# A two-layer hybrid trunk on one core: weight splits further ahead, and work queued in another order

## The chip, the cores and the metric

The kernel runs as one program on one core of one Trainium2 chip. The metric is the device time of one execution in microseconds (us). The kernel before takes 1798.98 us, the median of 3 runs (1797.5 to 1801.09). The engines are TensorE (PE for matmuls, PEld for its weight loads), VectorE (DVE), ScalarE (ACT), GpSimd (POOL) and SyncE (SP), which issues the transfers here. Every engine works through its own list of instructions in order.

## What is computed

Two layers over 512 tokens of width 1024, all in float32. Cut to what matters:

```python
for l in range(2):
    sh1, sc1, gt1, sh2, sc2, gt2 = split(silu(c) @ w_mod[l] + b_mod[l])
    h = rms_norm(x, g_pre1) * (1 + sc1) + sh1
    gu, gv, q, k, v, qi, ki, wi, lx, lg = split(h @ w_in)
    y_a = gelu(gu) * (block_mix(layer_norm(gelu(gv))) + b)     # gMLP, blocks of 128
    y_b = attention(rope(q), rope(k), v, keys=top128(indexer(qi, ki, wi)))
    y_c = gelu(lg) * linear_recurrence(causal_conv4(lx))        # RG-LRU
    g_a, g_b, g_c = split(sigmoid(h @ w_gate + b_gate))
    merged = g_a * (y_a @ w_br[0]) + g_b * (y_b @ w_br[1]) + g_c * (y_c @ w_br[2])
    x = x + gt1 * rms_norm(merged @ w_o, g_post1)
    h2 = rms_norm(x, g_pre2) * (1 + sc2) + sh2
    z_g, z_v = split(causal_conv3(h2 @ w_up))                   # 2816 + 2816 columns
    x = x + gt2 * rms_norm((silu(z_g) * z_v) @ w_down, g_post2)
```

## The kernel before

**Units of weights.** The tokens stand in four blocks (`TB`) of 128. All weights come as a stream of 143 units for each layer, each a tile of 128x1024, in the order of `unit_names` (L39): 4 `lx`, 4 `qi`, 1 `ki`, 4 `lg`, 4 `gv`, 4 `gu`, the 12 of `branch(2)`, 4 `v`, 4 pairs of `k` and `q`, the 12 of `branch(0)`, the 12 of `branch(1)`, 8 `wo`, 44 `up`, 22 `dn`. A branch has two `gate` units and one `br` unit, four times.

**Split products.** A product in float32 is made of three matmuls (`mm3`, L128 to L132): both operands are split into a rounded high part and the rest, and high x high (L130), high x low (L131) and low x high (L132) are summed in PSUM, with weights and activations in either role. A unit is 24 such matmuls. The weights' split is made on the way: `W.conv` (L162) has ACT copy the landed tile `wst` to `wh` (L109) and DVE subtract it, giving `wl` (L112). `W.get` (L191) emits the splits up to `LA` = 3 units ahead of the unit it hands out; there are `RB` = 5 pairs of buffers and 6 landing tiles. All other tiles of 128x512 (`S`, L93) come from one pool of `NS` = 46. Activations are split in the same way into `hh` and `hl` or two `S` tiles.

**Background work.** Between units the code calls `B.pump` (L213), a slot: it lets generators emit a few instructions each. Those are the recurrence (`lru`), the indexer with its top-k search (`indexer`, L519: rounds of MAX8 at L560 and MATCH_REPLACE8 at L562, then the ties and one last bias tile), the gMLP mixing, the attention (`attention`, L674), the modulation rows of later phases (`mod_task` and `mod_fin`, L299 and L321, among the "low" tasks) and the next layer's small parameters (`prepare`). A generator that yields -n isn't called again for n slots. `B.drain` (L232) pumps until nothing is left; it stands before the first `br` unit of `branch(1)`, which needs the attention's result, and at the end of the layer's two halves.

**Attention.** 16 steps (head, block), one a slot. `score` (L678) is a matmul, a masked maximum on DVE (L685), an Exp on ACT (L106) and a scaling on POOL (L116); `flip` (L697) is the transposes on PE (L702) and a copy to `S` on ACT (L109); `values` (L707) the matmuls with `v`. In slot n the code emits score n, then flip n-2, then values n-3. The score of block i needs the indexer's bias i; the last one, bias 3, is the longest search.

**Token phases.** `wo` and `dn` (`tok_phase`, L397) hold all eight PSUM banks. Their last `TAIL` = 8 units are gone through token block by token block, so that a block's chain of norms (`chain`, L440: two sums of squares on ACT, `rsqrt` on POOL at L240, DVE for the rest) lies beside the next block's matmuls. For that, 8 units must be split at once: `W.conv` fills `wh`/`wl`, and `W.extra` splits three more into `S` tiles; then the activations that the tail needs are split (`hl_of`). After the last block, five units of the next phase are begun for half of the tokens (`start_half`, L373), between them the transposes of blocks 2 and 3 (`norm_out`, L354), then finished.

**Startup.** ACT sums the squares of `x`'s four blocks, and for each DVE and POOL make the factor; DVE accumulates the modulation row `acc` from eight tiles `m` (`mod_acc`, L293: L116 and L121).

## Time and profile before

| | us |
|---|---|
| median of 3 runs | 1798.98 |
| the profiled execution | 1798.2 |
| its span | 1796.4 |
| PE busy | 1720.5 (96%) |
| DVE busy | 1111.9 (62%) |
| ACT busy | 711.3 (40%) |
| POOL busy | 323.5 (18%) |

A matmul's bar covers the pipeline's depth, so the busy time of PE says that it nearly always has work, not that it runs at its peak. An idle time in the timeline stands in brackets with what ended it. PEclk is the granted clock of TensorE as a share of full speed; its mean over the run is 0.983. At full clock the 512-column matmuls of a unit follow each other every 0.227 us, at half clock every 0.427 us. Line numbers are those of the kernel before.

### The profile page before, as it was taken

The page shows a single profiled execution, that of the slowest core. Times are in us where ns is not written, and L with a number is a line of the kernel's source. Part 1 is how long each engine was busy: PE and PEld are TensorE (multiplying, and loading weights), DVE is VectorE, ACT ScalarE, POOL GpSimd, SP SyncE. Part 2 cuts the span into 40 slices and gives each one's busy share as a digit, 9 for nine tenths or more (in the row PEclk, how much of TensorE's full clock was granted, in tenths as well). Part 3 has the DMA queues.
Part 4 walks back from the last instruction along what each step waited for, and adds up shares of the span by engine and source line. Part 5 has one row for each costly group of instructions (what it writes and reads, how often), then busy time and mean ns, then how long its engine had stood idle before and what let it go on. Part 6 is the DMA issues. An engine that isn't in the chain of part 4 may idle for free.

```text
span 1796.4 us, 20845 instructions
## 1 busy us (share of the span) xinstructions
PE 1720.5 (96%) x7972; PEld 1421.0 (79%) x7972; DVE 1111.9 (62%) x1631; ACT 711.3 (40%) x1087; POOL 323.5 (18%) x248
## 2 busy tenths in 40 slices
PE   3999999899999999999999899998999999999998
PEld 1877888688889788888787688876888888888876
DVE  6738798844466888563465578986445676445442
ACT  3484323433343334342335643243333344334331
POOL 3241101632000112110003201044200012111000
PEclk8899999999999999999999999999999999999999
DMA  8424334432423666333234253444224153333311
GB/s 333 141 83 163 126 125 140 138 118 71 139 85 120 187 211 189 103 110 103 71 118 129 94 166 116 134 148 128 94 76 170 59 179 126 102 98 94 112 53 47
DMA packets 67643, 224.57 MB, mean 125 GB/s; under 512 B 7636, under 2 KB 8020, under 8 KB 67416
## 3 DMA queue, kind: packets, MB, share of 16 engines
q1 hardware_dynamic: 67248, 223.10, 38.8%
q8 instruction: 62, 1.02, 0.2%
q14 instruction: 37, 0.30, 0.1%
q10 hardware_dynamic: 296, 0.14, 0.0%
HBM read 219.02 MB, written 4.19 MB: 124 GB/s over the span
## 4 chain that ended last, share of the span: by engine, by line
PE 72%; DVE 12%; ACT 7%; issue 3%; DMA 3%; POOL 1%; SPq 0%; ACTq 0%; DVEq 0%; POOLq 0%
PE ps L132 23%; PE ps L131 23%; PE ps L130 23%; DVE wl L112 3%; PE ps L126 3%; DVE acc L121 2%; DVE s L121 2%; ACT s L104 2%; ACT s L109 2%; ACT wh L109 2%; DVE s L112 2%; POOL s L112 1%; DMA s<-in_rows_dram 1%; ACT L104 1%; DVE m L560 1%
## 5 line engine op out<-in xcount | busy, mean ns | idle before, releaser
L130 PE MATMUL ps<-hh,wh 128*128 128x512 f32 (+1 forms) x1608 | 606.0, 377 | 2.2 <-ACT wh L109 2.2
L132 PE MATMUL ps<-hh,wl 128*128 128x512 f32 (+1 forms) x1608 | 601.8, 374 | 2.9 <-DVE wl L112 2.8
L131 PE MATMUL ps<-hl,wh 128*128 128x512 f32 (+1 forms) x1608 | 601.4, 374 | 2.4 <-DVE hl L112 2.4
L112 DVE TENSOR_TENSOR wl<-wst,wh 128x1024 fp32r<-128x1024 f32 x273 | 350.2, 1286 | 317.5 <-ACT wh L109 315.9
L132 PEld LDWEIGHTS ps<-hh,wl 128*128 128x128 f32 x1608 | 303.2, 189 | 59.0 <-DVE wl L112 5.0
L131 PEld LDWEIGHTS ps<-hl,wh 128*128 128x128 f32 x1608 | 303.3, 189 | 57.1 <-DVE hl L112 3.4
L130 PEld LDWEIGHTS ps<-hh,wh 128*128 128x128 f32 x1608 | 303.5, 189 | 56.5 <-ACT wh L109 3.1
L109 ACT ACTIVATE wh<-wst 128x1024 fp32r<-128x1024 f32 x274 | 286.2, 1051 | 142.2 <-PE ps L132 104.8
L112 POOL TENSOR_TENSOR s<-s,s 128x512 f32<-128x512 f32 (+1 forms) x126 | 218.4, 1741 | 545.1 <-DVE s L121 422.5
L121 DVE SCALAR_TENSOR_TENSOR s<-ps,lw,s 128x511 f32<-128x511 f32 (+3 forms) x208 | 154.7, 747 | 92.6 <-ACT s L104 89.0
L130 PE MATMUL ps<-wh,s 128*128 128x512 f32 x384 | 151.1, 394 | 4.1 <-ACT s L109 4.1
L132 PE MATMUL ps<-wh,s 128*128 128x512 f32 x384 | 151.0, 393 | 2.2 <-DVE s L112 2.2
L131 PE MATMUL ps<-wl,s 128*128 128x512 f32 x384 | 151.1, 394 | 0.4 <-DVE wl L112 0.4
L104 ACT ACTIVATE s<-ps,lw 128x512 f32<-128x512 f32 x112 | 83.2, 761 | 131.9 <-PE ps L132 131.8
L240 POOL TENSOR_TENSOR sm<-sm,mhalf 128x1 f32<-128x1 f32 x40 | 22.4, 561 | 513.7 <-DVE sm L118 483.6
L109 ACT ACTIVATE s<-s 128x512 fp32r<-128x512 f32 (+2 forms) x100 | 59.9, 617 | 112.1 <-DVE s L112 65.0
L104 ACT ACTIVATE s<-ps,bg 128x512 f32<-128x512 f32 x48 | 33.0, 688 | 155.7 <-PE ps L132 155.7
L121 DVE SCALAR_TENSOR_TENSOR acc<-ms,cact,acc 128x1024 f32<-128x1024 f32 x70 | 93.5, 1336 | 0.0
L130 PEld LDWEIGHTS ps<-wh,s 128*128 128x128 f32 x384 | 72.9, 190 | 20.1 <-ACT s L109 5.0
L132 PEld LDWEIGHTS ps<-wh,s 128*128 128x128 f32 x384 | 72.9, 190 | 18.2 <-DVE s L112 3.1
L104 ACT ACTIVATE s<-s 128x512 f32<-128x512 f32 x52 | 32.4, 631 | 136.8 <-DVE s L121 136.7
L131 PEld LDWEIGHTS ps<-wl,s 128*128 128x128 f32 x384 | 72.7, 189 | 16.4 <-DVE wl L112 1.3
(128 smaller groups left out, 1937.4 us busy)
## 6 DMA issues: line engine op xcount, KB each, us to landing
wst<-in_wu_dram SPq DMA_DIRECT2D x286, 512.0 KB, 3.8
ms<-in_wm_dram SPq DMA_DIRECT2D x80, 512.0 KB, 4.0
s<-in_rows_dram SPq DMA_DIRECT2D x34, 256.0 KB, 6.1
m<-in_wm_dram SPq DMA_DIRECT2D x16, 512.0 KB, 8.5
s<-in_x_dram SPq DMA_DIRECT2D x16, 256.0 KB, 5.6
xd<-s SPq DMA_DIRECT2D x8, 256.0 KB, 2.0
s<-xd SPq DMA_DIRECT2D x8, 256.0 KB, 6.3
out_dram<-s SPq DMA_DIRECT2D x8, 256.0 KB, 2.1
```

The lines of the kernel that those rows point to most:

```text
L104: A_.activation(o, i, f, bias=bias, scale=scale)
L109: A_.activation(o, i, AF.Copy, scale=scale)
L112: (eng or V).tensor_tensor(o, a, b, op)
L121: V.scalar_tensor_tensor(o, a, s, b, op0=op0, op1=op1)
L126: T_.matmul(o, l, r, start=start, stop=stop)
L130: T_.matmul(o, lh, rh, start=start, stop=False)
L131: T_.matmul(o, lh, rl, start=False, stop=False)
L132: T_.matmul(o, ll, rh, start=False, stop=stop)
L240: G_.tensor_tensor(y, h, mhalf, ALU.pow)
L560: V.max(m, cur[:, :n])
```

## The change

`RB` goes to 6, `LA` to 5 and `NS` to 42. The four `v` units and their copies to `S` stand right behind `ki`, ahead of `lg`. Attention emits flip and values of a slot ahead of its score, and a score waits until slot `at + 4` (it was 3) and two slots behind the emission of its bias. The split of `ya`, which was four ACT copies and four POOL subtractions in one go ahead of `branch(0)`, is a background task of ACT and DVE, one each two slots. In the token phases' tails activation splits and weight splits alternate; `sumsq` is cut in two, and the second half (`rstd`, on DVE and POOL) is queued behind one more weight split in `chain`; the same cut in the startup puts two steps of `acc` ahead of the four `rstd`. The low tasks pause while half units are carried; `mod_fin` and `lru` start later by two slots and one, `prepare` by up to twelve; Silu of a gate tile is queued behind the second convolution. The code of `lg` and of the two loads for gMLP is the same behind the `v` units and left out below.

```diff
@@ -39,6 +39,7 @@
 def unit_names():
     n = [("lx", j) for j in range(4)]
     n += [("qi", j) for j in range(4)] + [("ki", 0)]
+    n += [("v", t) for t in range(4)]
     n += [("lg", j) for j in range(4)]
     n += [("gv", t) for t in range(4)] + [("gu", j) for j in range(4)]
...
     n += branch(2)
-    n += [("v", t) for t in range(4)]
     for j in range(4):
         n += [("k", j), ("q", j)]
...
-    RB = 5
-    LA = 3
-    NS = 46
+    RB = 6
+    LA = 5
+    NS = 42
...
-        def add(self, gen, first=False):
-            self.tasks.insert(0 if first else len(self.tasks), [gen, 0])
+        def add(self, gen, first=False, wait=0):
+            self.tasks.insert(0 if first else len(self.tasks), [gen, self.slot + wait])
 
         def pump(self, budget):
             self.slot += 1
-            if self.low and self.slot % self.every == 0:
+            if self.low and not carry and self.slot % self.every == 0:
...
+    carry = []
     B = Bg()
...
     def mod_fin(l, v, key, acc):
-        yield -2
+        yield -4
...
@@ -337,6 +338,9 @@
         s = small(2)
         for i, a in enumerate(srcs):
             act(junk, a, AF.Square, acc=s[:, i:i + 1])
+        return s
+
+    def rstd(s):
         h = small(1)
         ts(h, s[:, 0:1], s[:, 1:2], D * EPS, AD, AD)
         return rsqrt(h)
...
         W.hold = W.cur
-        W.conv(W.cur + RB)
-        W.extra(TAIL - RB)
         W.aside = TAIL - RB
-        a_, w_ = [], []
-        for k in range(nk - TAIL, nk):
-            a_.append(hl_of(k))
-            w_.append(W.take())
+        a_ = []
+        for k in range(TAIL):
+            a_.append(hl_of(nk - TAIL + k))
+            if W.ncv < W.cur + RB:
+                W.conv(W.ncv + 1)
+            elif W.ncv < W.cur + TAIL:
+                W.extra(1)
+        w_ = [W.take() for _ in range(TAIL)]
...
         def chain(tb, more=lambda: None):
             scaled(tb)
-            y1[tb] = sumsq(ps[tb])
+            y1[tb] = rstd(sumsq(ps[tb]))
             more()
             resid(tb)
             if nxt:
                 more()
-                y2[tb] = sumsq(xs[tb])
+                q = sumsq(xs[tb])
                 more()
+                y2[tb] = rstd(q)
                 normed(tb)
...
-        y1[2] = sumsq(ps[2])
+        y1[2] = rstd(sumsq(ps[2]))
...
-                y2[2] = sumsq(xs[2])
+                y2[2] = rstd(sumsq(xs[2]))
...
             ts(gt[:, :n], gt[:, :n], -NEG, None, M)
-            res[i] = gt
+            res[i], ready[i] = gt, B.slot
             yield 1.4
 
     def lru(xc, lw, s84, wts, gl, res):
         rr, ii = [], []
-        yield -2
+        yield -3
...
-    def attention(qk, at, v, bias, res):
+    def attention(qk, at, v, bias, ready, res):
...
         for n in range(len(pairs) + 3):
-            if n < len(pairs):
-                hd, i = pairs[n]
-                while len(qk) <= hd or B.slot < at[hd] + 3 or i not in bias:
-                    yield -1
-                score(hd, i)
             if 2 <= n < len(pairs) + 2:
                 flip(*pairs[n - 2])
             if n >= 3:
                 values(*pairs[n - 3])
+            if n < len(pairs):
+                hd, i = pairs[n]
+                while len(qk) <= hd or B.slot < at[hd] + 4 or i not in bias or B.slot < ready[i] + 2:
+                    yield -1
+                score(hd, i)
             yield 1.0
             yield -1
...
+        v = []
+        for p in tok_units("v"):
+            o = S()
+            copy(o, p)
+            v.append(o)
+
+        for t in range(4):
+            p = col("lg")
+            o = S()
+            act(o, p, AF.Gelu_apprx_tanh)
+            gl.append(o)
+            B.pump(3.0)
...
         mix = gmlp_mix(lw, vh, u, ws, bs, ya)
+        yas = []
+
+        def split_ya():
+            for _ in range(4):
+                yh, yl = S(F32R), S(F32R)
+                split(yh, yl, ya.pop(0))
+                yas.append((yh, yl))
+                yield -2
         B.add(mix, True)
...
-        v = []
-        for p in tok_units("v"):
-            o = S()
-            copy(o, p)
-            v.append(o)
         yb = [None] * 4
         qk, at = [], []
-        B.add(attention(qk, at, v, bias, yb), True)
+        B.add(attention(qk, at, v, bias, ready, yb), True)
+        while len(ya) < 4:
+            B.pump(3.0)
+        B.add(split_ya(), True)
         for j in range(4):
             kk = rope(col("k"), cos_a, sin_a)
             B.pump(2.0)
@@ -893,12 +910,10 @@
             at.append(B.slot)
             B.pump(2.0)
         v = kk = None
-        for g in range(4):
-            yh, yl = S(F32R), S(F32R)
-            split(yh, yl, ya[g], G_)
-            ya[g] = (yh, yl)
-        branch(0, ya, False, False, 2.5)
-        del ya[:]
+        while len(yas) < 4:
+            B.pump(3.0)
+        branch(0, yas, False, False, 2.5)
+        del yas[:]
...
-            B.add(prepare(l + 1))
+            B.add(prepare(l + 1), wait=12)
...
             zg = conv3(col("up"), j)
-            act(zg, zg, AF.Silu)
             B.pump(1.5)
             zv = conv3(col("up"), FT + j)
+            act(zg, zg, AF.Silu)
             tt(zg, zg, zv, M, G_)
             aj.append(zg)
             B.pump(1.5)
...
-    ys = [sumsq(xs0[tb]) for tb in range(TB)]
+    sq = [sumsq(xs0[tb]) for tb in range(TB)]
     g0 = []
...
+    acc = one.tile([P, 1024], F32, tag="acc", name=nm("acc"))
+    for k in range(KT):
+        mod_acc(acc, m0.pop((1, k)), k)
+        if k == 1:
+            ys = [rstd(q) for q in sq]
     for tb in range(TB):
         for hf in range(2):
             act(xs0[tb][hf], xs0[tb][hf], AF.Identity, scale=ys[tb])
-    acc = one.tile([P, 1024], F32, tag="acc", name=nm("acc"))
-    for k in range(KT):
-        mod_acc(acc, m0.pop((1, k)), k)
```

**ACT at the start of `branch(0)`, layer 0.** Before, in its order: the tanh of a gate, the Exp of score (head 0, block 3), the copy of the flipped tile of (0, 1), a weight split, the next gate, and the Exp of (1, 0).

```order
L104 ACTIVATE s_2660<-ps_2629,bg_77_327 128x512
L106 ACTIVATE s_2667,sm_2672<-s_2667,sm_2670 128x512
L109 ACTIVATE s_2680<-ps_2677 128x256
L109 ACTIVATE wh_2685<-wst_2470 128x1024
L104 ACTIVATE s_2715<-ps_2684,bg_77_327 128x512
L106 ACTIVATE s_2719,sm_2724<-s_2719,sm_2722 128x128
```

Now, ACT at the same place: the copy of (0, 1), weight splits and gates, and then the Exp of (0, 3).

```order
L109 ACTIVATE s_2633<-ps_2630 128x256
L109 ACTIVATE wh_2646<-wst_2423 128x1024
L104 ACTIVATE s_2676<-ps_2645,bg_83_339 128x512
L109 ACTIVATE wh_2685<-wst_2482 128x1024
L104 ACTIVATE s_2715<-ps_2684,bg_83_339 128x512
L109 ACTIVATE wh_2717<-wst_2534 128x1024
L106 ACTIVATE s_2758,sm_2763<-s_2758,sm_2761 128x512
```

The copy of the flipped tile stood behind the Exp, and stands six instructions ahead of it.

**ACT ahead of the last eight `dn` units, layer 0.** Before: one activation split (`s<-s`), three weight splits to `wh`, three in halves (`s<-wst`), and then the other activation splits.

```order
L109 ACTIVATE s_6595<-s_5664 128x512
L109 ACTIVATE wh_6599<-wst_6467 128x1024
L109 ACTIVATE wh_6629<-wst_6501 128x1024
L109 ACTIVATE wh_6635<-wst_6535 128x1024
L109 ACTIVATE s_6641<-wst_6569 128x512
L109 ACTIVATE s_6645<-wst_6569 128x512
L109 ACTIVATE s_6651<-wst_6603 128x512
L109 ACTIVATE s_6655<-wst_6603 128x512
L109 ACTIVATE s_6661<-wst_6633 128x512
L109 ACTIVATE s_6665<-wst_6633 128x512
L109 ACTIVATE s_6671<-s_5736 128x512
```

Now, ACT at the same place:

```order
L109 ACTIVATE s_6603<-s_5659 128x512
L109 ACTIVATE wh_6607<-wst_6475 128x1024
L109 ACTIVATE s_6637<-s_5731 128x512
L109 ACTIVATE wh_6641<-wst_6509 128x1024
L109 ACTIVATE s_6647<-s_5816 128x512
L109 ACTIVATE s_6651<-wst_6543 128x512
L109 ACTIVATE s_6655<-wst_6543 128x512
L109 ACTIVATE s_6661<-s_5888 128x512
```

The second activation split stood ten instructions behind the first, and stands two behind it.

**PE ahead of the first `br` unit of `branch(1)`, layer 0.** Before, PE ends the attention so: flips of (3, 2) with values of (3, 1), then the flips of (3, 3), then values; the score of (3, 3) stands a unit earlier, 27 rows above.

```order
L126 MATMUL ps_3353<-s_2555,s_2599 128x512
...
L702 MATMUL ps_3405<-ks,s_3298 128x128 x3
L126 MATMUL ps_3370<-s_3368,s_2201 128x128
L126 MATMUL ps_3370<-s_3368,s_2203 128x128
L702 MATMUL ps_3413<-ks,s_3355 128x128 x4
L126 MATMUL ps_3370<-s_3409,s_2201 128x128
```

Now, PE behind the same unit: the flip of (3, 0), values of (2, 3), the score of (3, 2) (128x384), the flip of (3, 1), values, the score of (3, 3) (128x512), the flip of (3, 2), values; the flip of (3, 3) follows.

```order
L707 MATMUL ps_3374<-ks,s_3276 128x128
L126 MATMUL ps_3216<-s_3324,s_956 128x128
L126 MATMUL ps_3216<-s_3324,s_958 128x128
L126 MATMUL ps_3216<-s_3324,s_960 128x128
L126 MATMUL ps_3216<-s_3324,s_962 128x128
L126 MATMUL ps_3386<-s_2563,s_2626 128x384
L707 MATMUL ps_3398<-ks,s_3331 128x128 x2
L126 MATMUL ps_3403<-s_3376,s_956 128x128
L126 MATMUL ps_3405<-s_2563,s_2626 128x512
L707 MATMUL ps_3417<-ks,s_3388 128x128 x3
L126 MATMUL ps_3403<-s_3401,s_956 128x128
L126 MATMUL ps_3403<-s_3401,s_958 128x128
```

The last two scores stand between the flips that lead to the `br` unit, with no unit of matmuls between a score and its flip.

## Rows read from the trace of the kernel before

**Rows 1.** Page, span and busy time of each engine.

```profile
span 1796.4 us, 20845 instructions
...
PE 1720.5 (96%) x7972; PEld 1421.0 (79%) x7972; DVE 1111.9 (62%) x1631; ACT 711.3 (40%) x1087; POOL 323.5 (18%) x248
```

**Rows 2.** Waits of PE: what, releaser, us in total, times, longest.

```profile
PE ps L126 <- ACT s L109: 13.8, 3, 6.3
```

**Rows 3.** Windows: start:end, us, busy by engine, PEclk, DMA share, GB/s.

```profile
132.70:139.70 7.00, 6.27 (x15) 4.92 (x16) 6.09 (x8) 6.93 (x9) 0.00 (x0) 0.51 0.25 77
...
876.80:880.40 3.60, 3.60 (x10) 2.79 (x10) 2.67 (x5) 0.43 (x1) 0.00 (x0) 0.53 0.08 25
...
1228.40:1235.40 7.00, 4.53 (x13) 3.75 (x14) 3.20 (x11) 4.42 (x9) 2.16 (x2) 0.51 0.68 207
```

**Rows 4.** PE timeline, start, us, instruction, [idle before <-releaser]: `lg`, `gv`.

```profile
132.17 0.50 PE L130 MATMUL ps<-wh,hh 128*128 128x512 f32 x1 [2.06 <-ACT wh L109]
...
133.43 0.80 PE L131 MATMUL ps<-wl,hh 128*128 128x512 f32 x1 [0.76 <-DVE wl L112]
...
154.27 0.49 PE L131 MATMUL ps<-wl,hh 128*128 128x512 f32 x1 [0.80 <-DVE wl L112]
...
975.89 1.12 PE L126 MATMUL ps<-s,s 128*128 128x512 f32 x2 [1.31 <-ACT s L104]
...
1032.29 0.50 PE L131 MATMUL ps<-wl,hh 128*128 128x512 f32 x1 [1.16 <-DVE wl L112]
```

**Rows 5.** ACT timeline, unit `lg` of layer 0.

```profile
121.60 1.04 ACT L109 ACTIVATE wh<-wst 128x1024 fp32r<-128x1024 f32 x1
122.66 1.28 ACT L104 ACT_TABLE_LOAD   x1
```

**Rows 6.** PE timeline, the start of attention.

```profile
309.92 0.49 PE L126 MATMUL ps<-s,s 128*128 128x128 f32 x2 [1.09 <-POOL s L112]
...
352.55 1.23 PE L126 MATMUL ps<-s,s 128*128 128x128 f32 x4 [6.28 <-ACT s L109]
...
1230.87 1.22 PE L126 MATMUL ps<-s,s 128*128 128x128 f32 x4 [6.26 <-ACT s L109]
```

**Rows 7.** Timelines of DVE, ACT and POOL, score of head 0, block 3.

```profile
350.50 0.68 DVE L685 CUSTOM_DVE_ANT_0 s<-ps,s 128x512 f32<-128x512 f32 x1
...
351.41 0.72 ACT L106 ACTIVATE s<-s,sm 128x512 f32<-128x512 f32 x1 [11.67 <-DVE sm L687]
...
352.60 1.56 POOL L116 TENSOR_SCALAR s<-s,sm 128x512 f32<-128x512 f32 x1 [5.35 <-DVE sm L691]
```

**Rows 8.** PE timeline, the start of the feed-forward part.

```profile
589.83 0.50 PE L130 MATMUL ps<-hh,wh 128*128 128x512 f32 x1 [0.35 <-ACT wh L109]
...
628.81 0.50 PE L132 MATMUL ps<-hh,wl 128*128 128x512 f32 x1 [1.74 <-DVE wl L112]
```

**Rows 9.** PE timeline, the last eight `dn` units of layer 0.

```profile
874.68 0.50 PE L130 MATMUL ps<-wh,s 128*128 128x512 f32 x1 [2.07 <-ACT s L109]
...
876.52 0.50 PE L132 MATMUL ps<-wh,s 128*128 128x512 f32 x1 [1.10 <-DVE s L112]
```

**Rows 10.** DVE timeline, the startup.

```profile
17.53 0.74 DVE L116 TENSOR_SCALAR acc<-m,cact 128x1024 f32<-128x1024 f32 x1
18.31 9.21 DVE L121 SCALAR_TENSOR_TENSOR acc<-m,cact,acc 128x1024 f32<-128x1024 f32 x7
```

**Rows 11.** PE timeline before `branch(1)`'s first `br` unit, layer 0.

```profile
431.11 1.02 PE L126 MATMUL ps<-s,s 128*128 128x512 f32 x2
...
437.90 0.49 PE L702 MATMUL ps<-ks,s 128*128 128x128 f32 x3
```

**Rows 12.** Timelines of DVE and PE at the end of `wo`, layer 0.

```profile
548.54 1.22 DVE L112 TENSOR_TENSOR wl<-wst,wh 128x1024 fp32r<-128x1024 f32 x1
...
552.79 0.69 DVE L112 TENSOR_TENSOR s<-s,mod 128x512 f32<-128x512 f32 x1
...
554.82 1.04 PE L358 MATMUL ps<-ks,s 128*128 128x128 f32 x8
```

More of the change, by code (lines that the diff above doesn't have):

```diff
@@ L369, in cm @@
             mm3(ps[:, c0:c0 + n], w(k * P, P), hs(k, c0, n), k == 0, k == KT - 1)
-    carry = []
     def start_half():
@@ L517, in rope, with indexer @@
         return d
-    def indexer(qi, kih, wr, res):
+    def indexer(qi, kih, wr, res, ready):
         yield -2
@@ L793, in layer, with tok_units @@
         B.pump(2.0)
-        bias = {0: bias0}
-        idx = indexer(qi, kih, wr, bias)
+        bias, ready = {0: bias0}, {0: 0}
+        idx = indexer(qi, kih, wr, bias, ready)
         del qi, kih, kr, k0, k1, kp, wr, r, a, c
         B.add(idx)
+        def tok_units(kind):
+            ps = [bank() for _ in range(TB)]
+            for t in range(4):
+                w = W.get(kind)
+                for tb in range(TB):
+                    for i in range(2):
+                        k = 2 * t + i
+                        mm3(ps[tb], hs(k, tb * P, P), w(i * 512, 512), k == 0, k == KT - 1)
+                if t < 3:
+                    B.pump(3.0)
+            return ps
+        v = []
[3 more added lines that the diff above has]
+            v.append(o)
         for t in range(4):
@@ L811, in layer @@
         nc.sync.dma_start(bs, bass.AP(tensor=srcb.tensor, offset=srcb.offset, ap=[[0, P], [1, 512]]))
-        def tok_units(kind):
-            ps = [bank() for _ in range(TB)]
-            for t in range(4):
-                w = W.get(kind)
-                for tb in range(TB):
-                    for i in range(2):
-                        k = 2 * t + i
-                        mm3(ps[tb], hs(k, tb * P, P), w(i * 512, 512), k == 0, k == KT - 1)
-                if t < 3:
-                    B.pump(3.0)
-            return ps
         vh = []
```

## Prediction

> **What bounds the kernel now.** I read the busy times first, then the waits of PE, then the windows for its clock, then the timelines around each wait. PE is busy for 96% of the span, 1720.5 of 1796.4 us, and no other engine is near it [rows 1]. So the time is the matmuls, plus the stretches where PE stands, plus those where it runs at half clock. PE's idle times over 0.25 us sum to 67.8 us in its timeline: 28.1 in the startup, 39.7 later. The largest class is "ACT s", 13.8 us in three waits [rows 2]: PE waits for a copy that ACT makes in order. After most of the long idle times the granted clock is 0.51 for some 7 us, or 0.53 for 3.6 us [rows 3], which is the lower of its two levels, 1.2 GHz. A stretch of the first kind costs 7.00 x (1 - 0.51) = 3.4 us, one of the second 3.60 x (1 - 0.53) = 1.7 us. There are four of the first after the startup, at 132.7, 351.2, 1009.9 and 1228.4, and two of the second, at 876.8 and 1747.2. A change pays here only where it removes a wait of PE, and then twice if the clock had fallen behind it.
>
> **The change, part by part.** The sums go against the profiled execution, 1798.2 us (span 1796.4), 0.8 below the median shown.
>
> *Look-ahead and `v` moved, at `lg` and `gv`.* In layer 0 PE waits 2.06, 0.76 and 0.80 us for the weights' parts [rows 4], and the first two are followed by a half-clock stretch: 3.6 + 3.4 = 7.0. In layer 1 six waits between 975.89 and 1032.29 (first 1.31, last 1.16) sum to 8.3, with one such stretch: 11.7. The cause is ACT. A weight copy takes 1.04 us, but between them ACT changes tables eight times from 95 to 138 us, each 1.28 us [rows 5], with the recurrence's Sigmoid and Sqrt against the units' Gelu. The copies are emitted only three units ahead. Five units ahead give two units of slack more, some 11 us at 5.44 us a unit, and the `v` units, which ask only four plain copies of ACT, give four units in which it catches up. A backlog of about 3 us is covered either way: I take all 18.7. If the backlog only moves, nothing of it comes; that is a rival.
>
> *Start of attention.* PE waits 1.09 us for POOL's rotary result and 6.28 us for the flipped tile's copy [rows 6]. That copy stood behind an Exp which was ready only at 351.41 and for which ACT idled 11.67 us [rows 7], since DVE was still in the indexer's last search. Now the copy is ahead of the Exp, and the score waits two slots behind its bias. In layer 1 the same two are 1.45 and 6.26. The four sum to 15.1, and two half-clock stretches add 6.8: 21.9. What is late next is DVE: its backlog is the same, and it gets four subtractions of `ya`, each about 0.69 us, in place of POOL. The first flip can then still wait for a score that DVE has not reduced. I count 1 us a layer against the change, 2.0 in all (0 if DVE is level, and up to the whole 21.9 back if not).
>
> *Start of the feed-forward part.* From 589.83 to 628.81 PE waits four times, 0.35 + 0.53, 1.24 and 1.74 us [rows 8], for weights and for a modulation row whose work came just ahead of them. The low tasks now pause while units are carried, `mod_fin` comes two slots later, and look-ahead covers the rest: 3.9.
>
> *Tails of `dn`.* PE waits 2.07 and 1.10 us [rows 9] in the third unit of the tail, since its activation split stands behind ten copies of weights on ACT; the clock then falls for 3.6 us. The alternating order puts it two instructions behind the first. 2.07 + 1.10 + 1.7 = 4.9 in each of two layers, 9.7. Some lateness can stay with a later unit; I take 0.3 a layer off, 0.6.
>
> *Startup.* DVE's chain over `acc` begins at 17.53 and is followed without idle to the first unit. Two of its steps, 0.74 and 9.21/7 = 1.3 us [rows 10], now run while ACT still squares: 2.0 (0 if their tiles land only then; a gain cannot exceed the two steps).
>
> *Drain ahead of `branch(1)`'s first `br`.* This is what the change adds. Before, the last score is on PE at 431.11, a unit ahead of the flips at 437.90 [rows 11], and PE doesn't wait. Now the scores of (3, 2) and (3, 3) both stand in the drain, and flips follow them with no unit between. Such a score costs, from DVE's start at 350.50 to POOL's end at 352.60 + 1.56, 3.7 us [rows 7] with ACT's Exp between. Say the unit ahead ends at T. Flip and values of (3, 0) and (2, 3) take PE to T + 1.6; the score of (3, 2) is through POOL at about T + 5.7; the next, behind it on the same three engines, at T + 8.2 (the distance is POOL's 1.56 and the share of Exp and sum that can't overlap). PE has the rest done by T + 3.3. It waits 2.4 us for the flip of (3, 2), 1.5 for that of (3, 3), and 0.7 behind ACT's copies for the last values: 4.6 in all, in pieces. Behind PE stand the `br` unit's matmuls, so nothing hides it. Does the clock fall? In `lg`, a wait of 2.06 us and one of 0.76 shortly behind it were enough [rows 3, 4]; 4.6 us in this form is more, so I add 3.4: 8.0 a layer. In layer 1 `mod_fin` falls into the drain too, four matmuls of 0.23 us and a wait for a row from DRAM. No row shows it there; the nearest is the 1.74 us for which a row held DVE and so PE [rows 8]. With 0 and 3.5 us as ends I take 2.0: 10.0 in layer 1. Together 18.0; the ends are 0, if the last units cover it, and 25.
>
> The Trainium skill bears on this step ("TensorE: Matmul & The Clock Gate", section "Why this matters for your kernels"): it says to keep idle gaps between matmul bursts short, since long ones put the array back to half rate. By that the drain's gaps, none above 2.5 us, would cost only themselves, and the sum would be 6.8 us less. The trace does not bear it out here: 2.06 and 0.76 us sufficed.
>
> *Chain of the fourth block in `wo` and `dn`.* The second `rstd` is now queued behind one more weight split on ACT and DVE. The subtraction is 1.22 us, and its copy stands 1.04 ahead [rows 5, 12]. The block's norm was done at 553.48 (552.79 + 0.69), and PE wanted it at 554.82 [rows 12]: 1.3 us of slack. Some 2.1 us later it would be 0.8 late. In three token phases (the last has no next) that is 2.4, with 0 and 6 as ends.
>
> *The rest*, at nothing. Fewer `S` tiles: 42 are used again only after more than a unit, in which their readers are done. Silu behind the second convolution: ACT is busy 40%, and the product is wanted many units later. `lru` a slot later: its result is needed only in `branch(2)`. If that cover is gone, each costs a wait of about 1 us a layer. Weight landings don't move: the six landing tiles are as before.
>
> The sum: gains 18.7 + 21.9 + 3.9 + 9.7 + 2.0 = 56.2; losses 18.0 + 2.4 + 2.0 + 0.6 = 23.0. 1798.2 - 33.2 = 1765.0.
>
> **The rivals.**
>
> *A. The drains cost only their idle time.* The clock stays at its upper level, 2 x 3.4 less: 1758. For it: the gaps are apart from each other by flips and values. Against it: rows 3 and 4, as above.
>
> *B. DVE's backlog takes the place of the Exp.* The attention's first flips wait for scores behind the search. For it: the 11.67 us of rows 7, and no DVE work goes away; the light `v` units that stood ahead of `k` and `q` are gone from there. Against it: a score is now two slots behind its bias. With half of the 21.9 back the time is 1776; with all of it 1787.
>
> *C. The look-ahead is earlier in the order, not in time.* ACT works in order, so a copy queued two units earlier behind the same table changes starts where it did. Then the 18.7 and 3.9 stay and the time is 1765.0 + 22.6 = 1788. For it: ACT has no idle time from 118 to 138 us in layer 0. Against it: ACT is busy 40% over the span [rows 1], and the `v` units come just there.
>
> *D. Slower: the new order makes PE wait at a flip in every slot, and the attention runs at half clock throughout.* Flip and values now head each slot, in front of the score. If POOL's scaled tile isn't there, each of the 16 steps of a layer puts an idle time of a microsecond or so between units, and the clock doesn't come back. The stretch is some 95 us a layer (from 346 to 441), so at 0.5 it costs up to 47 a layer, 95 in all: 1860. It decides once more than 33 / 0.5 = 67 us of half clock come in. For it: one wait of 6.28 in such a place already gave 0.51 [rows 3, 6]. Against it: 3.7 us of work on a score against two units, 10.9 us, until its flip.
>
> **How the numbers follow.** The forecast has 0.55, A 0.15, B 0.12, C 0.09, D 0.06, and 0.03 stay for a time near that of before, several of B, C and the ends of the drain together. The predicted time is 1765. The range goes from 1748 (A, with the losses of 5.0 in chain, flips and tail gone and half of the drains' idle hidden) to 1787 (B in full, nearly C). What a measurement of this kernel can tell from no change is 0.2%, 3.6 us. Forecast, A, B and C are all faster by more: 0.91. Within 0.2%: 0.03. Slower: D, 0.06.
>
> **What would show it.** In the waits of PE, "ACT s" at L126 and "ACT wh" at L130 should be gone or under 2 us in all. PEclk should be full at `lg`, at the start of attention and in the `dn` tails. In their place, flips in the drain ahead of `branch(1)` should wait for POOL's scaling (L116), some 4 to 5 us a layer, with a half-clock stretch behind; if the clock is full there, A holds. The first step of `acc` should start near 11 to 13 us. Transposes at L358 waiting for DVE at the end of `wo` show the chain's term. Waits at `lg` and `gv` of the old size are C, idle times at the first flips with DVE as releaser B, and a clock of 0.5 over the whole attention D. The forecast is wrong if the drain is covered, or if DVE, at 62% the second busiest engine, cannot take the subtractions where they now stand.

## The result, and the profile after

| | before | after |
|---|---|---|
| median of 4 runs, us | 1799.49 (1797.5 to 1801.09) | 1773.99 (1771.54 to 1777.18) |
| ratio, 95% interval | | 0.986 (0.9841 to 0.9879) |
| profiled execution, us | 1798.2 | 1777.18 |

The change gives 25.5 us; 33 were forecast, and the time lies in the stated range. The profiled execution of after is the slowest of its four, so its trace shows 21.0 us of difference. The page after:

```profile
span 1775.4 us, 20874 instructions
...
PE 1712.5 (96%) x7972; PEld 1420.1 (80%) x7972; DVE 1119.8 (63%) x1635; ACT 703.1 (40%) x1075; POOL 309.2 (17%) x240
```

PE still bounds it [rows 1]. Its waits after (what, releaser: us in total, times, longest):

```profile
PE ps L707 <- POOL s L116: 23.0, 6, 10.6
...
PE ps L126 <- ACT s L104: 2.7, 1, 2.7
PE ps L131 <- DVE hl L112: 2.5, 3, 0.9
PE ps L130 <- ACT s L104: 1.2, 1, 1.2
```

The 13.8 us for ACT's copies [rows 2] are gone, and so are all waits for weights' parts. In their place stands one class: a flip (now L707) that waits for POOL's scaling of a score (L116), six times. The PE timeline after, at two places in layer 0: the start of attention, and the drain.

```profile
326.01 0.47 PE L707 MATMUL ps<-ks,s 128*128 128x128 f32 x1 [10.61 <-POOL s L116]
...
432.84 0.55 PE L707 MATMUL ps<-ks,s 128*128 128x128 f32 x3 [2.47 <-POOL s L116]
...
434.98 1.11 PE L707 MATMUL ps<-ks,s 128*128 128x128 f32 x4 [1.15 <-POOL s L116]
```

In layer 1 the same are 4.89, 1.54 and 2.35 us:

```profile
1188.92 0.47 PE L707 MATMUL ps<-ks,s 128*128 128x128 f32 x1 [4.89 <-POOL s L116]
```

The windows after (start:end, us, busy by engine, PEclk, DMA share, GB/s): the first two behind the waits of layer 0, the last two over the stretches that hold `lg` and `gv` of layer 0, and the `dn` tail of layer 0 with `lg` and `gv` of layer 1:

```profile
317.80:331.50 13.70, 5.49 (x13) 4.02 (x14) 10.97 (x22) 6.45 (x11) 6.38 (x5) 0.50 0.37 115
433.80:440.70 6.90, 5.75 (x24) 5.33 (x24) 0.70 (x2) 2.25 (x4) 1.13 (x1) 0.51 0.01 2
60.00:315.40 255.40, 255.40 (x1147) 209.92 (x1145) 195.87 (x319) 111.50 (x161) 51.94 (x42) 1.00 0.43 136
440.70:1188.00 747.30, 737.44 (x3521) 617.72 (x3519) 504.60 (x706) 301.24 (x447) 107.93 (x83) 1.00 0.41 130
```

At `lg` and in the `dn` tail the clock is now full, where it was 0.51 and 0.53 [rows 3]. By place, idle time of PE in both traces:

| place | before, us | after, us |
|---|---|---|
| first unit of layer 0 starts at | 50.36 | 47.71 |
| `lg`, `gv`, layers 0 + 1 | 3.6 + 8.3 | 0 + 3.8 |
| start of attention | 7.4 + 7.7 | 10.6 + 4.9 |
| drain ahead of `br` | 0 + 0 | 3.6 + 3.9 |
| start of feed-forward | 3.9 | 0 |
| `dn` tails | 3.2 + 3.2 | 0 + 0 |

So everything went as forecast in its direction except the largest term, the start of attention: nothing gained there. The question for the experiments is why.

The timelines after show what stood ahead of the first score, whose matmul PE began at 303.61: PE's row of it, the rows of DVE, and last a row of POOL that ran beside DVE's first subtraction.

```profile
303.61 0.38 PE L126 MATMUL ps<-s,s 128*128 128x128 f32 x2
...
303.61 1.78 DVE L112 TENSOR_TENSOR s<-s,s 128x512 fp32r<-128x512 f32 x1
306.65 0.69 DVE L121 SCALAR_TENSOR_TENSOR s<-ps,s 128x512 f32<-128x512 f32 x1 [1.26 <-DMA s<-in_rows_dram]
308.28 0.69 DVE L121 SCALAR_TENSOR_TENSOR mod<-s,s 128x512 f32<-128x512 f32 x1 [0.94 <-DMA s<-in_rows_dram]
...
310.71 0.69 DVE L121 SCALAR_TENSOR_TENSOR s<-ps,s 128x512 f32<-128x512 f32 x1 [1.74 <-DMA s<-in_rows_dram]
...
321.01 1.75 DVE L112 TENSOR_TENSOR s<-s,s 128x512 fp32r<-128x512 f32 x1
322.69 0.28 DVE L690 CUSTOM_DVE_ANT_0 s<-ps,bias 128x128 f32<-128x128 f32 x1
...
302.63 2.21 POOL L112 TENSOR_TENSOR s<-s,s 128x512 f32<-128x512 f32 x1 [2.29 <-issue]
```

The score is taken up at 322.69, 19 us after its matmul. In between are `mod_fin`'s waits for rows from DRAM (3.9 us) and two of `ya`'s subtractions, 1.78 and 1.75 us. I had priced such a subtraction at 0.69 us, from a row without POOL beside it. Before, DVE took the first score up earlier, though PE reached it later, at 309.92 [rows 6]:

```profile
318.85 0.28 DVE L685 CUSTOM_DVE_ANT_0 s<-ps,bias 128x128 f32<-128x128 f32 x1
```

So the lag grew from both ends: PE came 6.3 us earlier, after its gains in the startup and at `lg`, and DVE 3.8 us later.

### The profile page after: what moved, and what is told of

Read it like the earlier page. It is cut to its first block, busy times and chain, and to the rows that moved or that the text cites. A ratio compares the mean times of both kernels' runs of the same rounds, so it can differ in the third digit from the quotient of the medians.

```text
span 1775.4 us, 20874 instructions
## 1 busy us (share of the span) xinstructions
PE 1712.5 (96%) x7972; PEld 1420.1 (80%) x7972; DVE 1119.8 (63%) x1635; ACT 703.1 (40%) x1075; POOL 309.2 (17%) x240
## 4 chain that ended last, share of the span: by engine, by line
PE 75%; DVE 15%; ACT 3%; issue 3%; DMA 2%; POOL 1%; SPq 0%; DVEq 0%; POOLq 0%; ACTq 0%
PE ps L130 24%; PE ps L131 24%; PE ps L132 24%; PE ps L126 3%; DVE wl L112 3%; DVE m L565 2%; DVE s L112 2%; DVE s L567 2%; DVE acc L121 2%; DVE s L121 2%; ACT wh L109 1%; DMA s<-in_rows_dram 1%; POOL s L112 1%; ACT s L104 1%; ACT s L109 1%
## 5 line engine op out<-in xcount | busy, mean ns | idle before, releaser
L112 DVE TENSOR_TENSOR wl<-wst,wh 128x1024 fp32r<-128x1024 f32 x277 | 356.1, 1289 | 264.3 <-ACT wh L109 264.1
L109 ACT ACTIVATE wh<-wst 128x1024 fp32r<-128x1024 f32 x278 | 291.3, 1052 | 171.5 <-PE ps L132 104.6
L112 POOL TENSOR_TENSOR s<-s,s 128x512 f32<-128x512 f32 (+1 forms) x118 | 201.5, 1715 | 585.5 <-DVE s L121 371.3
L130 PE MATMUL ps<-wh,s 128*128 128x512 f32 x416 | 162.4, 390 | 0.0
L132 PE MATMUL ps<-wh,s 128*128 128x512 f32 x416 | 161.9, 389 | 0.0
L131 PE MATMUL ps<-wl,s 128*128 128x512 f32 x416 | 161.8, 389 | 0.0
L132 PEld LDWEIGHTS ps<-wh,s 128*128 128x128 f32 x416 | 78.1, 188 | 16.2
L130 PEld LDWEIGHTS ps<-wh,s 128*128 128x128 f32 x416 | 78.1, 188 | 16.0
L131 PEld LDWEIGHTS ps<-wl,s 128*128 128x128 f32 x416 | 78.1, 188 | 16.0
L109 ACT ACTIVATE s<-ps 64x512 f32<-64x512 f32 (+6 forms) x104 | 55.7, 543 | 68.3 <-PE ps L132 35.9
```

The source lines that it names most:

```text
L109: A_.activation(o, i, AF.Copy, scale=scale)
L112: (eng or V).tensor_tensor(o, a, b, op)
L130: T_.matmul(o, lh, rh, start=start, stop=False)
L131: T_.matmul(o, lh, rl, start=False, stop=False)
L132: T_.matmul(o, ll, rh, start=False, stop=stop)
```

## The experiments

The theory from this trace: the first flips wait because DVE, which has no idle time left while the indexer searches, carries its stalls and added work up to the first score. The rival: the new order of flip and score does it. The experiments were timed in three groups, each beside the kernel before, whose median was 1798.3 to 1799.2 us in them and 1799.5 beside the changed kernel. So a difference from the changed kernel's 1773.99 is open by about 1 us, besides the intervals. Some of the edits below are shown shortened.

**e1_ya_pool: the subtractions of `ya` on POOL.**

```diff
-                split(yh, yl, ya.pop(0))
+                split(yh, yl, ya.pop(0), G_)
```

> The changed kernel, with the four subtractions of ya's split on POOL instead of DVE; still one every two slots. Theory (DVE's queue): PE's 10.61 us wait for the flip of (0, 0) in layer 0 comes from DVE reaching that score late, and two of the subtractions, 1.78 and 1.75 us, stand ahead of it. Without them the wait is 10.61 - 3.5 = 7.1 us in layer 0 and 4.9 - 3.5 = 1.4 in layer 1, time 1767. Rival (the order of flip and score): DVE's load does not matter, the waits stay at 10.6 and 4.9, time 1774.

Measured 1770.74 us, ratio 0.9839 (0.9822 to 0.9855). The interval overlaps that of the changed kernel, so the time alone tells little; the trace shows more. PE at the first flip of layer 0:

```profile
323.46 0.47 PE L707 MATMUL ps<-ks,s 128*128 128x128 f32 x1 [7.58 <-POOL s L116]
```

3.0 us less than 10.61, and in layer 1 2.88 in place of 4.89: DVE's load counts, and the two subtractions are somewhat under a third of the wait.

**e2_rows_early: `mod_fin`'s rows loaded ahead of its pause.**

```diff
     def mod_fin(l, v, key, acc):
+        ld = [mod_load(l, v, hf) for hf in range(2)]
         yield -4
...
-            mod_row(l, v, acc, hf, o)
+            mod_row(l, v, acc, hf, o, ld[hf])
```

Here `mod_row` is cut in two: `mod_load` issues the loads of the rows, and `mod_row` does the rest.

> The changed kernel, with the rows that mod_fin adds loaded before its pause of four slots instead of behind it. Theory (DVE's queue): DVE stands 1.26 + 0.94 + 1.74 = 3.9 us for these rows just ahead of the first score of layer 0; without that the flip's wait is 10.6 - 3.9 = 6.7 us, and a similar part goes in layer 1 and in layer 1's drain: time 1767. Rival (the order): the wait stays at 10.6; if anything the S tiles, held four slots longer, cost a few us: 1774 to 1778.

Measured 1765.29 us, ratio 0.981 (0.9795 to 0.9824): 8.7 us better than the changed kernel. PE's first flip, DVE's additions of the rows and its first score:

```profile
318.51 0.47 PE L713 MATMUL ps<-ks,s 128*128 128x128 f32 x1 [2.85 <-POOL s L116]
```

```profile
301.71 0.68 DVE L121 SCALAR_TENSOR_TENSOR s<-ps,s 128x512 f32<-128x512 f32 x1
...
315.19 0.28 DVE L696 CUSTOM_DVE_ANT_0 s<-ps,bias 128x128 f32<-128x128 f32 x1
```

The wait fell by 7.8 us, twice what I expected. DVE was 3.6 us ahead already before these rows: in the changed kernel an earlier `mod_fin` had held it 4.50 us for a row, and DVE had made up only 0.9 us of that by the subtraction at 303.61, which here stands at 299.99. DVE's row in the changed kernel:

```profile
204.18 0.69 DVE L112 TENSOR_TENSOR s<-ps,s 128x512 f32<-128x512 f32 x1 [4.50 <-DMA s<-in_rows_dram]
```

The theory holds, and more strongly than I had put it.

**e3_old_attn: attention's order and waiting as before.**

```diff
-            if 2 <= n < len(pairs) + 2: flip(...)
-            if n >= 3: values(...)
             if n < len(pairs):
-                while len(qk) <= hd or B.slot < at[hd] + 4 or i not in bias or B.slot < ready[i] + 2:
+                while len(qk) <= hd or B.slot < at[hd] + 3 or i not in bias:
                     yield -1
                 score(hd, i)
+            if 2 <= n < len(pairs) + 2: flip(...)
+            if n >= 3: values(...)
```

> The changed kernel, with attention's order and waiting as before (score ahead of flip and values, slot at + 3, no two slots behind the bias); all else as changed. Theory: the drains' 6.4 and 6.9 us go, since the last score is on PE a unit earlier again; DVE's backlog stays, so the first flips still wait about 8 to 12 us in layer 0, and the wait of 6.3 us at the flipped tile's copy behind the Exp of (0, 3) is back in both layers: 1774 - 13 + 18 = 1779. Rival (the new order makes the flips wait): the 10.6 goes altogether and 6.3 a layer returns, 1774 - 13 - 20 + 18 = 1759.

Measured 1774.59 us, ratio 0.9864 (0.9849 to 0.9878): the same as the changed kernel. PE's timeline, the first flip, and the copies behind the Exp of (0, 3) in both layers:

```profile
318.84 0.47 PE L707 MATMUL ps<-ks,s 128*128 128x128 f32 x1 [6.18 <-POOL s L116]
...
351.88 0.71 PE L126 MATMUL ps<-s,s 128*128 128x128 f32 x4 [2.12 <-ACT s L109]
...
1216.08 1.22 PE L126 MATMUL ps<-s,s 128*128 128x128 f32 x4 [8.91 <-ACT s L109]
```

The waits are redistributed: 6.2 and, in layer 1, 1.6 us at the first flips, less than the 8 to 12 that I expected in layer 0; 2.1 and 8.9 at the copies; and the drains shrink to 2.3 us a layer, where the theory had them vanish. Neither theory nor rival gives this. The order is not the cause of DVE's lag; it decides only who shows it. Undone, it costs as much as it gives, as long as DVE lags.

**e4_two_steps: two attention steps in the slot of the step ahead.**

```diff
             yield 1.0
-            yield -1
+            if n not in (8, 11):
+                yield -1
```

> The changed kernel, with two of attention's steps (behind steps 8 and 11) in the slot of the step ahead, so that the last score is emitted two slots earlier. Theory: the drains' waits of 2.47 + 1.15 and 1.54 + 2.35 us and their half-clock stretches go, 6.4 + 6.9 = 13 us: 1761; no new waits, since DVE has no search left in that stretch. Rival (PE waits for the doubled steps instead, because the flip of one is nearer behind its score): half of it comes back, 1767, or all, 1774.

Measured 1762.93 us, ratio 0.98 (0.9785 to 0.9814), 11.1 us better. The flips of (3, 2) and (3, 3) in layer 0 follow without a wait:

```profile
429.30 0.49 PE L707 MATMUL ps<-ks,s 128*128 128x128 f32 x3
...
430.07 0.60 PE L707 MATMUL ps<-ks,s 128*128 128x128 f32 x4
```

So the drains cost 11.1 us together, of which 7.5 are idle time; the other 3.6 are left for their two half-clock stretches. The first flips wait about as before (9.6 and 5.5 us), so this edit does nothing there.

**e5_ahead, e6_v_early, e7_tail: single parts, each on the kernel before.** Their edits:

```diff
-    RB = 5; LA = 3; NS = 46            # e5_ahead
+    RB = 6; LA = 5; NS = 42
...
+    n += [("v", t) for t in range(4)]  # e6_v_early: behind ("ki", 0), copies to S too
...
-        W.conv(W.cur + RB)             # e7_tail
-        W.extra(TAIL - RB)
+        for k in range(TAIL):
+            a_.append(hl_of(nk - TAIL + k))
+            if W.ncv < W.cur + RB: W.conv(W.ncv + 1)
+            elif W.ncv < W.cur + TAIL: W.extra(1)
```

> The kernel before, with RB 6, LA 5 and NS 42 alone. Theory (weights' parts are late only because they are queued three units ahead): the waits at lg and gv (3.6 us and a half-clock stretch in layer 0, 8.3 and one in layer 1) and at the start of the feed-forward part (3.9) go for the most part, about 18: 1781. Rival (the room comes from the v units moved there): ACT's queue is as full as before, the waits stay within 2 us of their size: 1797 to 1800.

Measured 1796.81 us, ratio 0.9988 (0.9979 to 0.9998). All waits for weights' parts are gone, and new ones of the same size stand elsewhere (PE timeline: the indexer's products, the first score, `mod_fin` in the feed-forward part):

```profile
182.68 0.69 PE L130 MATMUL ps<-s,s 128*128 128x384 f32 x1 [2.69 <-ACT s L104]
...
308.73 0.62 PE L126 MATMUL ps<-s,s 128*128 128x128 f32 x2 [3.78 <-POOL s L112]
...
609.47 1.95 PE L126 MATMUL ps<-s,onesr 128*128 128x512 f32 x3 [5.53 <-ACT s L109]
```

Nearly the rival's time, but neither mechanism as written. I read it so, from the releasers alone: a split that is queued earlier on ACT pushes other work behind it.

> The kernel before, with the four v units and their copies moved behind ki alone. Theory (look-ahead): the copies are still only three units ahead, but four units without Gelu stand where ACT has its backlog, so half of the 15 to 18 us of lg and gv goes; the attention starts with less room for DVE, some us come there: 1790 to 1797. Rival (the v units give the room): lg and gv lose all their waits, 1799 - 18 = 1781.

Measured 1783.37 us, ratio 0.9916 (0.9901 to 0.9931): 15 us, near the rival's time. Waits at `lg` and `gv` are 0.7 us in layer 0 and 4.0 in layer 1, where they were 3.6 and 8.3, with three units of look-ahead as before; so not all of them went, and some of the gain came elsewhere (2.2 us of waits at the start of the feed-forward part in place of 3.9). The traces show what the place of `v` does for ACT: from 85 to 185 us it loads a table eight times before and in e5, but four times here and in the changed kernel. Each load is 1.28 us [rows 5].

> The kernel before, with the alternating order of activation and weight splits ahead of the tails alone. Theory: the waits of 2.07 and 1.10 us and the half-clock stretch go in both dn tails, nothing else moves: 1799.2 - 9.7 = 1789.5. Rival (the weights, now later in the order, are late instead): the waits move to a later unit of the tail, 1797 to 1801.

Measured 1787.37 us, ratio 0.994 (0.9925 to 0.9955): 11.0 us, and no wait of PE is left in either tail. The theory holds; what lies above 9.7 is not resolved.

**e8_three: the edits of e1, e2 and e4 together on the changed kernel.**

> The changed kernel with three of the edits tried on it together: ya's subtractions on POOL, mod_fin's rows loaded before its pause, two attention steps in the slot of the step ahead. Theory (the waits add up, and what is left at the start of attention is DVE's): PE's waits for flips and their half-clock stretches go in both layers, 1774 - 11 (drains) - 9 (rows) - 5 (what is left, 2.9 + 3.0 us with half of it hidden) = 1749. Rival (each hides the next wait, so the gains overlap): no lower than 1757.

Measured 1742.83 us, ratio 0.9692 (0.9676 to 0.9708): more than the sum. Windows of e8_three at both places of layer 0, the drain and the start of attention:

```profile
410.00:430.00 20.00, 19.99 (x100) 16.41 (x99) 9.40 (x14) 7.88 (x13) 1.56 (x1) 1.00 0.21 72
312.00:332.00 20.00, 20.00 (x91) 16.38 (x90) 17.53 (x33) 12.15 (x22) 13.72 (x11) 1.00 0.40 128
```

PE has no idle time and full clock; no flip waits in either layer. Part of the excess over the sum of the single gains (3.2 + 8.7 + 11.1 us) fits what e2 left: waits of 2.85 and 3.02 us at the first flips, each with a half-clock stretch behind it, go altogether here. What is left is in layer 1 (2.64 us at the recurrence's matmuls):

```profile
950.53 0.89 PE L126 MATMUL ps<-s,s 128*128 128x512 f32 x1 [2.64 <-ACT s L104]
```

**e9_fin_two: `mod_fin`'s pause two slots, as before, in the changed kernel.**

```diff
-        yield -4
+        yield -2
```

> The changed kernel, with mod_fin's pause two slots as before instead of four. Theory (mod_fin now falls just ahead of the first score): two slots earlier DVE has 11 us more to catch up with its waits for rows, the flip's wait of 10.6 us in layer 0 falls to 3 to 6 us, and up to 2 us come back at the start of the feed-forward part: 1768 to 1771. Rival (in DVE's order the same work still stands ahead of the score): 10.6 stays, 1774.

Measured 1784.83 us, ratio 0.9914 (0.9898 to 0.9931), 10.8 us worse. PE at the first flip of layer 0, then in layer 1:

```profile
322.52 0.47 PE L707 MATMUL ps<-ks,s 128*128 128x128 f32 x1 [7.08 <-POOL s L116]
...
1169.88 0.73 PE L126 MATMUL ps<-s,onesr 128*128 128x512 f32 x2 [1.74 <-DVE s L112]
...
1197.95 0.47 PE L707 MATMUL ps<-ks,s 128*128 128x128 f32 x1 [7.48 <-POOL s L116]
...
1209.92 0.69 PE L707 MATMUL ps<-ks,s 128*128 128x128 f32 x2 [3.69 <-POOL s L116]
```

Both were wrong. Layer 0's wait falls by 3.5 us, but in layer 1 `mod_fin`'s own matmuls wait and the flips wait 11.2 in place of 4.9. The pause moves the stall and cannot take it away. Why layer 1 loses so much more than layer 0 gains stays open.

**e10_three_near: e8_three with RB 5, LA 3 and NS 46.** The edit is that of e5_ahead, backwards.

> The changed kernel with the three edits (POOL subtraction, early rows, two doubled steps), and RB 5, LA 3, NS 46 as before the change. Theory (look-ahead only decides which work in ACT's order is late; the room comes from the other edits): within 4 us of the version with look-ahead, 1743 to 1747, with small waits for weights' parts at lg in layer 1. Rival (look-ahead is needed once the other waits are gone): the waits at lg, gv and the feed-forward start are back, 5 to 12 us more, 1748 to 1755.

Measured 1740.15 us (1739.27 to 1740.22), ratio 0.9668 (0.9654 to 0.9683): the fastest, 59 us below before. Its span is 1738.4 us, and the clock is full from 50 us to the last 4 us. The longest wait of PE after the startup is for a weight's part, at `lg` in layer 1:

```profile
983.75 0.50 PE L132 MATMUL ps<-hh,wl 128*128 128x512 f32 x1 [1.53 <-DVE wl L112]
```

So the deeper look-ahead is worth nothing here. That it costs 2.7 us I can't claim, since the intervals overlap; the trace names a place, the recurrence's 2.64 us, which this kernel does not have.

**e11_lru_one: e8_three with the recurrence's first loop one block a slot.**

```diff
                 lst.append(o)
-            yield 1.2
+            yield 2.0
```

> The changed kernel with the three edits, and the recurrence's first loop one block a slot instead of two (cost 2.0 instead of 1.2). Theory (in layer 1 PE waits 2.64 us for a PSUM bank that a Sigmoid behind the indexer's splits on ACT must empty, with a half-clock stretch of 3.4 us behind): both go, 1742.8 - 2.6 - 1.7 = 1738.5. Rival (the recurrence ends two slots later and branch(2) waits for it): 1743 to 1748.

Measured 1763.43 us, ratio 0.9799 (0.9785 to 0.9814), 20.6 worse than e8_three. The wait it was to remove doubled, and the drain's came back (PE timeline):

```profile
423.78 0.55 PE L713 MATMUL ps<-ks,s 128*128 128x128 f32 x3 [2.60 <-POOL s L116]
...
971.48 2.07 PE L126 MATMUL ps<-s,s 128*128 128x512 f32 x2 [5.46 <-ACT s L104]
```

The slot's budget is shared, and a dearer generator delays the indexer: its search begins at 215.08, in e8 at 203.17 (DVE's first MAX8); the score of (0, 3) is taken up at 351.18, in e8 at 339.76; so the last scores come later. My rival had the sign, not the place.

**e12_v_late: the changed kernel with `v` where it was.** The edit is that of e6_v_early, backwards.

> The changed kernel with the v units back between branch(2) and k. Theory (the v units' place gives most of the gain at lg and gv): 10 to 15 us slower, 1784 to 1789, with ACT as releaser at lg and gv. Rival (with mod_fin and lru later, look-ahead alone covers lg and gv): 1774, or less, since the light v units ahead of k and q give DVE room again: 1765.

Measured 1775.8 us, ratio 0.9867 (0.9852 to 0.9882): no difference that can be told. The theory was wrong; the rival's 1774 fits. The first flip of layer 0 waits 3.9 us in place of 10.6, the indexer's products 3.5 and 3.3 us:

```profile
182.19 0.69 PE L130 MATMUL ps<-s,s 128*128 128x384 f32 x1 [3.50 <-ACT s L104]
...
325.19 0.36 PE L707 MATMUL ps<-ks,s 128*128 128x128 f32 x1 [3.92 <-POOL s L116]
```

No wait for a weight's part is at `lg` or `gv` here, so with the deeper look-ahead the place of `v` isn't needed for that. DVE's search begins and its first score is taken up so, in the changed kernel (first row) and here:

```profile
208.59 0.42 DVE L565 MAX8 m<-s 128x8 f32<-128x256 f32 x1
...
216.90 0.41 DVE L565 MAX8 m<-s 128x8 f32<-128x256 f32 x1
...
321.86 0.28 DVE L690 CUSTOM_DVE_ANT_0 s<-ps,bias 128x128 f32<-128x128 f32 x1
```

From the search to the score DVE takes 105.0 us here and 114.1 in the changed kernel (208.59 to 322.69): `v` behind `ki` frees ACT at `lg` and takes room from DVE at `k` and `q`. But here the search begins 8.3 us later, so the score comes only 0.8 us earlier; the flip waits less mainly because PE itself reaches it 5.9 us later.

## Why the prediction was right or wrong

*Start of attention: the step that failed.* I said that the copy ahead of the Exp frees PE, 21.9 us, and left DVE 2.0. The copy did come free (no L126 waits for ACT's copies), but PE then met the score itself: 10.6 + 4.9 us idle against 15.1 [rows 6], with half-clock stretches of 13.7 and 6.8 us against two of 7.0. That is rival B in full at this place, to which I gave 0.12. Its sign shows at one remove: the flips' releaser is POOL's scaling, and POOL waits for DVE. The error was to read ACT's 11.67 us [rows 7] as the fault of ACT's order, when DVE was what it waited for: e3 shows that the order only chooses who waits, e1 and e2 that DVE's load and its stalls for rows set the length, and e8 that with both gone PE doesn't wait (its third edit alone, e4, leaves 9.6 and 5.5 us there). My term for DVE, 2.0 us, missed three things: a subtraction beside POOL costs 1.75 to 1.79 us and not 0.69, DVE's stalls for rows, and that PE, with what it gained upstream, comes 6.3 us earlier to a score that DVE takes up 3.8 us later.

*Look-ahead and `v` at `lg` and `gv`.* Of 18.7 us, 3.8 of idle time stayed, none of it for a weight's part. I had read the first of layer 1's six waits, 1.31 us at 975.89 [rows 4], with the weights, but it is the recurrence's matmuls waiting for a Sigmoid on ACT, and it grew:

```profile
970.85 1.12 PE L126 MATMUL ps<-s,s 128*128 128x512 f32 x2 [2.66 <-ACT s L104]
```

The other 1.16 us is new, at the indexer's products. Of my two reasons one was credited wrongly: look-ahead alone gave 1.5 us (e5), `v` alone 15.0 (e6), and e10 needs no look-ahead. Nor are the two gains to be added: with the look-ahead in place, putting `v` back costs nothing that can be told (e12). Rival C had the time of look-ahead alone right, but not its way, since in e5 the waits for weights' parts did go, and others came.

*Start of the feed-forward part.* All four waits [rows 8] are gone, 3.9 us. It isn't the look-ahead: e5 has 5.5 us there, and e10, with the old look-ahead, none. Nor is it `mod_fin`'s two slots: e9 has none either. That leaves, of my reasons, the pause of the low tasks, which no run tested alone.

*Tails of `dn`.* Right: forecast 9.7 less 0.6, measured 11.0 alone (e7). (Nine weight copies stood ahead of the second activation split, not ten.)

*Startup.* Right in its mechanism: 2.0 forecast, 2.65 measured. That is more than the two steps, which I had called the most that a gain can be: the six steps behind them begin at 17.01, where the whole chain had begun at 17.53, and that half microsecond is not explained. The first step starts with its tile, at 11.23 (DVE timeline after, [rows 10] before):

```profile
11.23 0.75 DVE L116 TENSOR_SCALAR acc<-m,cact 128x1024 f32<-128x1024 f32 x1 [11.23 <-DMA m<-in_wm_dram]
13.45 1.28 DVE L121 SCALAR_TENSOR_TENSOR acc<-m,cact,acc 128x1024 f32<-128x1024 f32 x1 [1.46 <-DMA m<-in_wm_dram]
...
17.01 7.88 DVE L121 SCALAR_TENSOR_TENSOR acc<-m,cact,acc 128x1024 f32<-128x1024 f32 x6
```

*Drain.* The mechanism, the place and the fall of the clock were right; the sum was too high, 18.0 against 11.1 (e4). Idle time was 3.6 and 3.9 us against 4.6 and 6.6: layer 1's `mod_fin` cost at most the 0.3 between them, and a stretch at half clock costs less than I counted where PE stands in part of it. The same holds at the start of attention, where PE worked 4.53 of the 7.00 us at 1228.4 [rows 3] and 5.5 of the 13.7 after: I counted 3.4 us for each full stretch. Rival A falls: the granted clock is 0.51 behind 2.47 and 1.15 us.

*Chain of the fourth block.* 2.4 forecast, at most 1 measured. The norm did come 2 us later against PE (DVE row), but the eight transposes need its two halves one after the other, and started with the first (PE row; 1.38 us against 1.04 in [rows 12]):

```profile
552.90 0.69 DVE L112 TENSOR_TENSOR s<-s,mod 128x512 f32<-128x512 f32 x1
```

```profile
552.92 1.38 PE L362 MATMUL ps<-ks,s 128*128 128x128 f32 x8
```

Rival D did not come: the clock is full between the start of attention and the drain. Together, some 20 us too much gain at the start of attention and 4 at `lg` and `gv` were partly made good by 7 too much loss in the drains and smaller terms on that side. That the total came nearer than its largest step is luck.

## What to carry to other kernels

When an engine in order waits for another's result, moving the waiting instruction back shows the lag somewhere else; find the engine that has no idle time, and take its stalls away. An engine that waits in line for a transfer keeps the loss as long as it is saturated: issue the load ahead of the pause, not behind it (8.7 us in e2). And a look-ahead in an order of emission is no slack by itself: test it alone before giving it credit.

## What the runs showed of the hardware

A subtraction of `ya` on DVE, with both inputs in `S` tiles, took 1.75 to 1.79 us where a POOL TENSOR_TENSOR on two tiles was already running, all four times in layer 0. With none running the same instruction took 0.68 (layer 1, after):

```profile
1174.20 0.68 DVE L112 TENSOR_TENSOR s<-s,s 128x512 fp32r<-128x512 f32 x1
```

The Trainium skill ("SBUF — State Buffer", section "Who interferes with whom") says that a DVE instruction with two SBUF inputs contends with a GpSimd one that reads SBUF, and the trace agrees. I had moved this work to DVE in my sum at the undisturbed price.

The same wait does not always bring the granted clock down. PE's wait of 2.64 to 2.68 us at the recurrence's matmuls in layer 1 stands in the changed kernel and in seven of the experiments (e1 to e4, e8, e9, e12); the clock fell behind it, for 3.4 us, in e8 and e12 alone. The window of e8 (the changed kernel's, at 970.85, lies in the stretch 440.70:1188.00 of PEclk 1.00 above):

```profile
951.00:954.40 3.40, 3.40 (x8) 2.20 (x7) 1.21 (x1) 3.34 (x6) 0.00 (x0) 0.51 0.00 0
```

Behind 2.85 us it fell for 3.4 us (e2, layer 0), behind 2.47 and 1.15 us for 6.9, behind 10.6 us for 13.7; behind the single waits of 1.16 us (after, layer 1) and 1.53 us (e10) it did not.
